# Reordering the two mixers of a hybrid decoder: earlier attention scores, convolution taps at the gate's input, later norm factors and V transposes

## The chip, the cores and the metric

One core of a Trainium2 chip runs the whole program. The metric is the device time of one execution in microseconds (us); lower is better. Times of the kernel before are the median of three runs; its profile is one execution taken by the hardware profiler.

## The reference

Sixteen learned meta tokens are put ahead of 512 tokens of width 1024 (528 positions), and two layers are computed, each a mixer and an MLP, both with a norm ahead of them and one behind them. The output leaves the meta tokens out.

```python
a = rmsnorm(h, mix_pre_g[l])
proj = a @ w_in[l]                  # q 512, k 128, v 128, b 512, c 512, h 512
q = partial_rope(q, cos, sin); k = partial_rope(k, cos, sin)
y_attn = sliding_window_gqa_sinks(q, k, v, sinks[l])   # 8 q heads, 2 kv heads, window 128
y_conv = b_gate * conv(c_gate * hc, conv_w[l])         # depthwise, causal, 3 taps
y = concat(rmsnorm(y_attn, attn_out_g), rmsnorm(y_conv, conv_out_g))
h = h + rmsnorm(y @ w_out[l], mix_post_g[l])
m = rmsnorm(h, mlp_pre_g[l])
h = h + rmsnorm(relu(m @ w_up[l])**2 @ w_down[l], mlp_post_g[l])
```

All of it is float32. A softmax row of `y_attn` holds a query's 128 keys and one sink, which only adds to its denominator.

## The kernel before, in words

Activations lie transposed: 128 features on the partitions, tokens on the free axis, split into RA (tokens 0 to 271) and RB (272 to 527). In layer 1 the outputs of the meta tokens are not wanted any more, so most of its products take 256 or 258 columns of RA.

A float32 product is made of three passes on TensorE (PE): every weight tile and activation is split into a high part (ScalarE copies it, L107 for weights) and a low remainder (VectorE subtracts, L108), and L192 to L194 multiply high by high, low by high and high by low. One product, 128 outputs of one range, has eight pieces of the contraction and so 24 matmuls. "Cast" below means the pair L107/L108 for half a weight tile (128x512); all weights are cast on the chip, each while earlier products run.

A mixer runs in these stages:

- `first_tiles` (L412): the products of K, V and three of the four Q tiles for RA, then for RB, while the end of the layer's previous stage still delivers activations piece by piece (`Post.step`, L309, writes `a_lo` at L334). V's product is transposed back to token order by `later()` in `v_evac` (L584) and split into `vv`; `v_later[0]` and `v_later[1]` are these for RA and RB.
- `mixer` (L630) walks a list `plan` of 26 products: the fourth Q tile for RA and RB, then for two pairs of channels four products each of the conv's c gate, its input h and its b gate. Between them, by the table `between` that `put` fills, go the pieces of attention. For each of eight pairs n of a block of 128 queries and a kv head: S[n] the scores (eight matmuls, four masks with a row maximum on VectorE, four exps on ScalarE, and, one product later, the scaling of the four score blocks by the reciprocal sum, L655), T[n] eight transposes on PE (L695) and a split, A[n] the product with V. `SCORES_AT` is the index of the product behind which S[0] goes, and `PERIODS` the distances from one T to the next.
- The conv: `c_evac` (L754) scales the c gate into `us[j]`, `h_evac` (L762) multiplies the h product into it, and `b_evac` takes the three taps (three scaled copies on ScalarE, L773 and L776, two additions on VectorE, L777), multiplies by the b product (L779) and adds the square to the norm's sum (`add_sq`, L266: a square on ScalarE, an addition on VectorE, L276).
- `group_norm` (L783): a factor from the sum of squares (two matmuls with a tile of ones, L231; three activations; L244, L245), then for each of four tiles a multiplication with gain and factor (L795), a high copy on ScalarE and a low remainder (L798).
- the out-projection (L883): products on all eight normed tiles, the four of attention first, then the four of the conv (`act_y`). The first four products on RA run together, piece by piece of the contraction, 12 matmuls for each piece, and the norms of RB are put between these pieces as hooks (`{1: ..., 3: ...}`: behind the piece of that number).

`pend` is a list of closing steps that wait until the next product has been issued. The program is written as such a sequence, and a scheduler then fixes the order of each engine's instructions; the order it came to is what the chip runs. Each engine works through its own list in order, so an instruction that waits holds up all behind it.

Of the kernel before, what the change touches and what calls it, by code (L numbers as in the profile page):

```python
# [10 lines left out]
AF = mybir.ActivationFunctionType  # L11
ALU = mybir.AluOpType
# [8 lines left out]
NCH = 4  # L21
CAP, PCAP = 7, 5
NA = 5
SCORES_AT = 7
PERIODS = (2, 3, 2, 3, 2, 2, 2, 2)
EPS = 1e-6
NEG = -1.0e30
RA = (0, 272)
# [3 lines left out]
G_PRE, G_ATT, G_CONV, G_POST, G_MPRE, G_MPOST, G_CW, G_N = 0, 8, 12, 16, 24, 32, 40, 52  # L32
# [3 lines left out]
def trunk_kernel(ctx, tc, xT, gains, sinkb, sinkm, rope, masks, maskm, ident_in, w_in, w_out, w_up, w_down, outT):  # L36
    nc = tc.nc
    ACT, DVE, POOL, PE = nc.scalar, nc.vector, nc.gpsimd, nc.tensor
# [11 lines left out]
    def tmp(w=272):  # L50
        return tp.tile([P, 272], F32, tag="t", name="t", bufs=8)[:, :w]

    h = cp.tile([P, KT, L], F32, name="h")
    z = cp.tile([P, KT, L], F32, name="z")
# [10 lines left out]
    gt = cp.tile([P, 2, G_N], F32, name="gt")  # L65
# [112 lines left out]
    def wtiles(n):  # L178
        return [wtile() for _ in range(n)]
# [6 lines left out]
    def tile_done(most=9):  # L186
        taken[0] -= size(done[0])
        done[0] += 1
        refill(most)
# [23 lines left out]
    def gemm(item, act):  # L213
        for ev in mms([item], act):
            ev()
# [31 lines left out]
    def utile():  # L247
        return tp.tile([P, L + 2], F32, tag="u", name="u", bufs=2)
# [4 lines left out]
    pend = []  # L253

    def flush():
        while pend:
            pend.pop(0)()
# [28 lines left out]
    def pre_rstd(r, name):  # L286

        t0, t1 = r  # L290
        w = meansq(accs["h"][:, t0:t1], 0)
        if name not in held:
            hold(name)
        acc = accs[name][:, t0:t1]
        if name == "c":
            chain(w, rt[:, t0:t1])
            ACT.activation(acc, w, AF.Identity, scale=-8 * EPS, bias=epst[:, 2:3])
        else:
            ACT.activation(acc, w, AF.Square, scale=-2 * (8 * EPS) ** 0.5, bias=epst[:, 1:2])
# [112 lines left out]
    def first_tiles(act, pB, rA, rB, nxt):  # L412


        items, tables, after, pcap, norm = nxt
        w = wtiles(NA)
        iA, iB = items(w, 0), items(w, 1)
        evs = []

        def rstd_a():  # L420
            pre_rstd(rA, norm)
            tables(0)

        initial = isinstance(pB, Start)
        at = (2, 4) if initial else (3, 5)
        groups = [(i,) for i in range(NA)] if initial else [(0, 1, 2), (3,), (4,)]
        steps = iter(range(4))
        for group in groups:
            i = group[0]
            hooks = {}  # L430
            if i == 0:
                hooks = {1 if initial else 4: pB.start}
            if i == at[0]:
                hooks = {at[1]: rstd_a}
            if not initial:
                evs += mms([iA[j] for j in group], act, hooks)
            elif i == 0:
                evs += mms(iA[:2], act)
            elif i >= 2:
                evs += mms([iA[i]], act, hooks)  # L440

            ready = [evs] if initial else [evs[:3]] if i == at[0] else [[ev] for ev in evs]
            if i >= at[0]:
                for run in ready:
                    waiting = pend[:]
                    pend.clear()
                    for ev in run:
                        ev()
                    for f in waiting:
                        f()  # L450
                evs = [] if initial else evs[3:] if i == at[0] else []
            for n in (0, 1)[:1 if len(group) == 1 else 2]:
                m = next(steps, None)
                if m is not None:
                    pB.steps(m)
            after(group[-1])
        cap[0] = pcap
        evs = mms(iB[:3], act)
        pre_rstd(rB, norm)
        tables(1)  # L460
        flush()
        for ev in evs:
            ev()
            tile_done()
        for i in range(3, NA):
            waiting = pend[:]
            pend.clear()
            gemm(iB[i], act)
            for f in waiting:
                f()  # L470
            tile_done()
# [23 lines left out]
    def xrange(l):  # L495
        return (RA if l == 0 else XA, RB)
# [27 lines left out]
    class Mixer:  # L524
# [8 lines left out]
        def tables(self, n):  # L533

            t0, t1 = (RA, RB)[n]
            nc.sync.dma_start(ct[:, t0:t1], rope[0][:, t0:t1])
            nc.sync.dma_start(st[:, t0:t1], rope[1][:, t0:t1])
            ACT.activation(r2[:, t0:t1], rt[:, t0:t1], AF.Square)
            DVE.tensor_tensor(ct[:, t0:t1], ct[:, t0:t1], rt[:, t0:t1], ALU.mult)
            DVE.tensor_tensor(st[:, t0:t1], st[:, t0:t1], rt[:, t0:t1], ALU.mult)  # L540
            for sw in sws:
                POOL.memset(sw[:, t0:t1], 0.0)
# [78 lines left out]
        def items(self, w, n):  # L621
            r = (RA, RB)[n]
            return [(w[0], r, self.k_evac(n)), (w[1], r, self.v_evac(n)),
                    ] + [(w[2 + j], self.xr[n], self.q_evac(j, n)) for j in range(NA - 2)]

        def after(self, i):
            if i == NA - 1:
                self.v_later[0]()

    def mixer(l, mx, mlp_first):  # L630

        xr = xrange(l)
# [112 lines left out]
        us = {}  # L745
# [11 lines left out]
        def h_evac(j, r):  # L757
            t0, t1 = r

            def ev(ps):  # L760
                u = us[j][:, 2 + t0:2 + t1]
                DVE.tensor_tensor(u, u, ps, ALU.mult)  # L762
            return ev

        def b_evac(j, r):
            t0, t1 = r

            def ev(ps):
                n = t1 - t0
                w = [gt[:, l, G_CW + 4 * x + j:G_CW + 4 * x + j + 1] for x in range(3)]  # L770
                u = us[j]
                t = tmp(n)
                ACT.activation(t, u[:, 2 + t0:2 + t1], AF.Copy, scale=w[2])  # L773
                for x in (1, 0):
                    t2 = tmp(n)
                    ACT.activation(t2, u[:, x + t0:x + t1], AF.Copy, scale=w[x])  # L776
                    DVE.tensor_tensor(t, t, t2, ALU.add)  # L777
                y = z[:, 4 + j, t0:t1]
                DVE.tensor_tensor(y, t, ps, ALU.mult)  # L779
                add_sq("c", j == 0, y, r)  # L780
            return ev

# [30 lines left out]
        def attn_norm(n):  # L813
            return group_norm(0, 4, "a", G_ATT, xr[n])

        def conv_norm(n):
            return group_norm(4, 0, "c", G_CONV, xr[n])

        def at_once(steps):
            return lambda: [f() for f in steps]  # L820

        plan = [("q", j, n) for j in range(NA - 2, 4) for n in range(2)]
        for jp in range(2):
            for kind in "chb":
                t = [(kind, 2 * jp + m, n) for m in range(2) for n in range(2)]
                if kind == "b" and jp == 1:
                    t = [t[0], t[2], t[1], t[3]]
# [3 lines left out]
        def put(i, *fs):  # L831
            between.setdefault(i, []).extend(fs)
# [2 lines left out]
        S = [lambda i=i, g=g: scores(i, g) for i, g in order]  # L835
        T = [lambda i=i, g=g: transp(i, g) for i, g in order]
        A = [lambda i=i, g=g: attend(i, g) for i, g in order]
        put(1, mx.v_later[1])
        at = SCORES_AT
        put(at, S[0])  # L840
        put(at + 1, S[1])
# [4 lines left out]
        pos = at + 3  # L846
        for n in range(8):
            put(pos, T[n])
            put(pos + 1, A[n])
            if n == 3:  # L850
                put(pos + 1, lambda: attn_sums(xr[0]))
                put(pos + 3, *attn_norm(0))
            if n == 7:
                put(pos + 1, lambda: attn_sums(RB))
            if n + 2 < 8:
                put(pos + 1, S[n + 2])
            pos += PERIODS[n]
        put(len(plan) - 2, *conv_norm(0))
        tiles = {}
        for i, (kind, j, n) in enumerate(plan):  # L860
            if (kind, j) not in tiles:
# [13 lines left out]
        for i in sorted(between):  # L875
            for f in between[i]:
# [8 lines left out]
        refill()  # L885
        w = wtiles(6)
        evs = mms([(w[m], xr[0], z_evac(m, xr[0], False, True, (l, G_POST))) for m in range(4)], act_y,
                  {1: at_once(attn_norm(1)), 3: at_once(conv_norm(1))})
        for ev in evs:
            ev()  # L890
        for m in range(4, 6):
# [9 lines left out]
    def f_evac(m, r):  # L901
        t0, t1 = r

        def ev(ps):
            f = tmp(t1 - t0) if t1 - t0 <= 272 else utile()[:, :t1 - t0]
            DVE.tensor_scalar(f, ps, 0.0, None, ALU.max)
            ACT.activation(f, f, AF.Square)
            split(f_hi[:, m, t0:t1], f_lo[:, m, t0:t1], f)
        return ev
# [73 lines left out]

    def mlp_items(l):
        xr = xrange(l)
        return (lambda w, n: [(w[m], xr[n], f_evac(m, xr[n])) for m in range(NA)]), (lambda n: None), (lambda i: None), CAP, "z"

    def mlp(l, nxt, first):

# [33 lines left out]
            POOL.memset(t[:, :, :PAD].bitcast(F32), 0.0)  # L1023

    m0, m1 = Mixer(0), Mixer(1)
    first = [(m.items, m.tables, m.after, PCAP, "c") for m in (m0, m1)]
    sA, sB = Start(0, 0, RA, (0, 0)), Start(0, 0, RB, (0, 0))
    prep((lambda: sA.load(0), lambda: sA.steps(0), lambda: sA.load(1), lambda: sA.steps(1)))
    prep((lambda: sA.load(2), lambda: sA.steps(2), lambda: sA.load(3), lambda: sA.steps(3)))
# [77 lines left out]
```

## Time and profile before

| | us |
|---|---|
| median of 3 runs | 1130.06 |
| lowest and highest | 1129.5, 1130.84 |
| the profiled execution | 1129.28 |
| its span (first to last instruction) | 1127.5 |
| PE busy | 1083.7 (96%), 8066 matmuls and transposes |
| VectorE (DVE) busy | 821.8 (73%) |
| ScalarE (ACT) busy | 640.3 (57%) |
| mean granted clock of PE | 0.983 |

Times in the rows are microseconds from the start of the span. A matmul is listed with its whole duration, though the next one starts long before it ends: what one costs in a row of many is the distance between starts. The clock is given as a share of the full 2.4 GHz; 0.5 is the lower level, 1.2 GHz. "Idle before" is the time for which the engine stood still ahead of the row's instruction, and behind the arrow is what ended it.

### The profile page before, as it was taken

Reading aid. Unit: us, or ns where it says so; the run is one execution under the profiler, and the core shown is the slowest. Engines: PE = TensorE matmul, PEld = TensorE weight load, DVE = VectorE, ACT = ScalarE, POOL = GpSimd, SP = SyncE. Lnnn points to the kernel's source line nnn. Section 1 sums busy time; section 2 is a strip of 40 time slices with the busy share of each in tenths; the row PEclk is TensorE's granted clock in tenths of the full one; section 3 lists DMA queues with packets and bytes.
Section 4 is the critical chain, followed back from the end, with each engine's and each line's share of the span. In section 5 each row is a group of like instructions: output and inputs, shape, how many; then the busy total and the mean of one; then the engine's idle time right before and its main releaser. Section 6 shows DMA issues by size and latency. Waiting matters only on the chain.

```text
span 1127.5 us, 21429 instructions
## 1 busy us (share of the span) xinstructions
PE 1083.7 (96%) x8066; PEld 1039.0 (92%) x8066; DVE 821.8 (73%) x1943; ACT 640.3 (57%) x1542; POOL 11.1 (1%) x46
## 2 busy tenths in 40 slices
PE   9999889999999999999979998899999999999996
PEld 8999889999999999999978998799888988988995
DVE  7987867978486586586588888779955856856835
ACT  8665766665473274275356556666834724724732
POOL 2000000000000000000000000000000000000000
PEclk9999989999999999999999999899999999999998
DMA  8342122342243243144132321222422522522502
GB/s 248 85 130 60 38 75 59 93 131 71 61 130 97 66 123 113 49 121 132 38 93 60 106 75 39 76 67 85 131 75 73 152 75 68 157 75 69 147 1 75
DMA packets 197608, 102.04 MB, mean 91 GB/s; under 512 B 7360, under 2 KB 197456, under 8 KB 197504
## 3 DMA queue, kind: packets, MB, share of 16 engines
q1 hardware_dynamic: 196640, 99.88, 30.5%
q8 instruction: 63, 1.03, 0.4%
q10 hardware_dynamic: 688, 0.58, 0.1%
q14 instruction: 41, 0.34, 0.1%
q0 software_dynamic: 176, 0.21, 0.1%
HBM read 97.88 MB, written 2.10 MB: 89 GB/s over the span
## 4 chain that ended last, share of the span: by engine, by line
PE 87%; DVE 8%; ACT 3%; issue 1%; DMA 1%; SPq 0%; DVEq 0%; ACTq 0%
PE ps L194 27%; PE ps L193 27%; PE ps L192 27%; PE ps L198 2%; DVE acc L276 1%; PE ps L231 1%; DVE a_lo L334 1%; PE ps L695 1%; DVE h L323 1%; DVE wlo L108 1%; ACT S L649 1%; DMA h<-in_xT 0%; DVE t L320 0%; DVE p L280 0%; DVE t L322 0%
## 5 line engine op out<-in xcount | busy, mean ns | idle before, releaser
L193 PE MATMUL ps<-f_lo,whi 128*128 128x256 f32 (+2 forms) x1072 | 325.9, 305 | 0.0
L194 PE MATMUL ps<-f_hi,wlo 128*128 128x256 f32 (+2 forms) x1072 | 325.0, 305 | 0.0
L192 PE MATMUL ps<-f_hi,whi 128*128 128x256 f32 (+2 forms) x1072 | 323.5, 306 | 0.0
L193 PE MATMUL ps<-a_lo,whi 128*128 128x256 f32 (+3 forms) x808 | 234.7, 293 | 2.3 <-DVE a_lo L334 2.1
L192 PE MATMUL ps<-a_hi,whi 128*128 128x256 f32 (+3 forms) x808 | 231.7, 298 | 4.5 <-ACT a_hi L329 3.4
L194 PE MATMUL ps<-a_hi,wlo 128*128 128x256 f32 (+3 forms) x808 | 233.1, 291 | 0.0
L193 PEld LDWEIGHTS ps<-f_lo,whi 128*128 128x128 f32 x1072 | 201.6, 188 | 9.6
L194 PEld LDWEIGHTS ps<-f_hi,wlo 128*128 128x128 f32 x1072 | 201.8, 189 | 9.2
L192 PEld LDWEIGHTS ps<-f_hi,whi 128*128 128x128 f32 x1072 | 200.0, 188 | 9.4
L108 DVE TENSOR_TENSOR wlo<-wraw,whi 128x512 fp32r<-128x512 f32 x264 | 173.7, 688 | 44.6 <-ACT whi L107 23.2
L107 ACT ACTIVATE whi<-wraw 128x512 fp32r<-128x512 f32 x264 | 153.4, 622 | 87.9 <-PE ps L193 59.6
L193 PEld LDWEIGHTS ps<-a_lo,whi 128*128 128x128 f32 x808 | 156.2, 193 | 6.6 <-DVE a_lo L334 3.6
L192 PEld LDWEIGHTS ps<-a_hi,whi 128*128 128x128 f32 x808 | 152.3, 193 | 8.7 <-ACT a_hi L329 4.9
L194 PEld LDWEIGHTS ps<-a_hi,wlo 128*128 128x128 f32 x808 | 156.5, 194 | 1.4 <-DVE wlo L108 0.2
L507 DVE TENSOR_TENSOR z<-z,ps 128x272 f32<-128x272 f32 (+2 forms) x78 | 38.0, 487 | 100.1 <-PE ps L194 99.9
L193 PE MATMUL ps<-a_lo,wf 128*128 128x264 f32 (+1 forms) x384 | 107.9, 282 | 0.0
L107 ACT ACTIVATE wf<-wraw 128x512 fp32r<-128x512 f32 x96 | 59.7, 626 | 84.8 <-PE ps L193 51.7
L192 PE MATMUL ps<-a_hi,wf 128*128 128x264 f32 (+1 forms) x384 | 107.7, 282 | 0.0
L194 PE MATMUL ps<-a_hi,wf 128*128 128x264 f32 (+1 forms) x384 | 107.1, 282 | 0.0
L107 ACT ACTIVATE wf<-u 128x512 fp32r<-128x512 f32 x72 | 45.2, 628 | 88.1 <-PE ps L193 73.6
L108 DVE TENSOR_TENSOR wf<-wraw,wf 128x512 fp32r<-128x512 f32 x96 | 65.8, 689 | 11.6 <-ACT wf L107 10.4
L193 PEld LDWEIGHTS ps<-a_lo,wf 128*128 128x128 f32 x384 | 72.2, 188 | 0.1
(176 smaller groups left out, 1826.1 us busy)
## 6 DMA issues: line engine op xcount, KB each, us to landing
wraw<-in_w_up SPq DMA_DIRECT2D x128, 256.0 KB
wraw<-in_w_down SPq DMA_DIRECT2D x128, 256.0 KB
wraw<-in_w_in SPq DMA_DIRECT2D x72, 256.0 KB
wraw<-in_w_out SPq DMA_DIRECT2D x32, 128.0 KB
wraw<-in_w_out SPq DMA_DIRECT2D x16, 256.0 KB
h<-in_xT SPq DMA_DIRECT2D x4, 272.0 KB
h<-in_xT SPq DMA_DIRECT2D x4, 256.0 KB
outT<-h SPq DMA_DIRECT2D x8, 128.0 KB
```

The costliest lines, as they stand in the source:

```text
L107: ACT.activation(hi, raw, AF.Copy)
L108: DVE.tensor_tensor(lo, raw, hi.bitcast(F32), ALU.subtract)
L192: PE.matmul(ps, whi, ahi, start=first, stop=False, skip_group_check=onto)
L193: PE.matmul(ps, whi, alo, start=False, stop=False, skip_group_check=onto)
L194: PE.matmul(ps, wlo, ahi, start=False, stop=last, skip_group_check=onto)
L198: PE.matmul(ps, a[n], b[n], start=first and n == 0, stop=last and n == 1)
L231: PE.matmul(ps, ones[:, which, :], acc, start=True, stop=more is None)
L276: return (eng or DVE).tensor_tensor(acc, acc, sq, ALU.add)
L323: DVE.tensor_tensor(hk, hk, t, ALU.add)
L334: DVE.scalar_tensor_tensor(a_lo[:, k, t0:t1], hk, g, a_hi[:, k, t0:t1].bitcast(F32), ALU.mult, ALU.subtract)
L507: DVE.tensor_tensor(zz, zz, ps, ALU.add)
L649: ACT.activation(S[:, i, keys], S[:, i, keys], AF.Exp, bias=ng[:, i:i + 1], accum_out=dn[:, i:i + 1])
```

## The change

The scores start behind the fifth product of the plan, where it was the eighth, with other distances between the transposes; all eight pairs are so done some products before the plan's end. The taps move from `b_evac` to a closing step of `h_evac`; two of the three scaled copies on ScalarE are dropped, since VectorE now multiplies and adds in one instruction. The hook `after` of `first_tiles`, which transposed V of RA at its end, is gone: both V transposes stand in the plan, behind its first and third product. The attention norm of RA comes one product later, the conv norm of RA moves from the plan's last products into the out-projection's first hook, and the two norms of RB move to later hooks.

```diff
-SCORES_AT = 7
-PERIODS = (2, 3, 2, 3, 2, 2, 2, 2)
+SCORES_AT = 4
+PERIODS = (2, 2, 3, 2, 2, 3, 2, 2)
...
-            after(group[-1])
...
-        def after(self, i):
-            if i == NA - 1:
-                self.v_later[0]()
...
-                u = us[j][:, 2 + t0:2 + t1]
-                DVE.tensor_tensor(u, u, ps, ALU.mult)
+                u = us[j]
+                DVE.tensor_tensor(u[:, 2 + t0:2 + t1], u[:, 2 + t0:2 + t1], ps, ALU.mult)
+
+                def taps():
+                    w = [gt[:, l, G_CW + 4 * x + j:G_CW + 4 * x + j + 1] for x in range(3)]
+                    first = max(t0, xr[0][0])
+                    y = z[:, 4 + j, first:t1]
+                    ACT.activation(y, u[:, 2 + first:2 + t1], AF.Copy, scale=w[2])
+                    for x in (1, 0):
+                        DVE.scalar_tensor_tensor(y, u[:, x + first:x + t1], w[x], y, ALU.mult, ALU.add)
+                pend.append(taps)
...
-                n = t1 - t0
-                w = [gt[:, l, G_CW + 4 * x + j:G_CW + 4 * x + j + 1] for x in range(3)]
-                u = us[j]
-                t = tmp(n)
-                ACT.activation(t, u[:, 2 + t0:2 + t1], AF.Copy, scale=w[2])
-                for x in (1, 0):
-                    t2 = tmp(n)
-                    ACT.activation(t2, u[:, x + t0:x + t1], AF.Copy, scale=w[x])
-                    DVE.tensor_tensor(t, t, t2, ALU.add)
                 y = z[:, 4 + j, t0:t1]
-                DVE.tensor_tensor(y, t, ps, ALU.mult)
+                DVE.tensor_tensor(y, y, ps, ALU.mult)
                 add_sq("c", j == 0, y, r)
...
-        put(1, mx.v_later[1])
+        put(0, mx.v_later[0])
+        put(2, mx.v_later[1])
...
-                put(pos + 3, *attn_norm(0))
+                put(pos + 4, *attn_norm(0))
...
-        put(len(plan) - 2, *conv_norm(0))
...
-                  {1: at_once(attn_norm(1)), 3: at_once(conv_norm(1))})
+                  {0: at_once(conv_norm(0)), 4: at_once(attn_norm(1)), 6: at_once(conv_norm(1))})
```

The rows below are the orders of the engines' instructions (line, operation, output<-inputs, shape, and a count where equal ones follow each other). Lines of the changed kernel are up to five lower than those of the kernel before.

VectorE in layer 0 around the first softmax (S and mx: scores and their row maximum; wlo: the low half of a weight cast; u: a tile of c gate by h; names carry the scheduler's tile numbers). Before:

```order
L108 TENSOR_TENSOR wlo_1139<-wraw_1142,whi_1138 128x512
L644 TENSOR_TENSOR mx_1019<-mx_1019,sb_78 128x4
L645 TENSOR_SCALAR ng_1035<-mx_1019 128x4
L646 TENSOR_TENSOR se_1037<-sb_78,mx_1019 128x4
L762 TENSOR_TENSOR u_917<-u_917,ps_1046 128x272
L660 ISA S_1078,mx_1079<-ps_1081,mk_82 128x144
```

With the change:

```order
L639 TENSOR_TENSOR mx_921<-mx_921,sb_78 128x4
L108 TENSOR_TENSOR wlo_1104<-wraw_1105,whi_1103 128x512
L757 TENSOR_TENSOR u_840<-u_840,ps_1018 128x272
L655 ISA s_1050,mx_1051<-ps_1053,mkm_83 64x16
L655 ISA mx_1051 64x1
L108 TENSOR_TENSOR wlo_1104<-wraw_1107,whi_1103 128x512
L655 ISA s_1050,mx_1051<-ps_1057,mkm_83 64x16
L655 ISA mx_1051 64x1
L639 TENSOR_TENSOR mx_991<-mx_991,sb_78 128x4
L640 TENSOR_SCALAR ng_937<-mx_921 128x4
L641 TENSOR_TENSOR se_939<-sb_78,mx_921 128x4
```

Before, the sink's maximum (L644) was followed at once by the negated maximum that the exps need (L645); now two casts, a multiplication of the conv, the two masks of the meta tokens and the maximum of the second pair stand between these two (L639, L640).

VectorE at the end of layer 0's mixer, up to the conv norm of RA (z: conv or attention outputs; acc: sum of squares; L244 and L245 before are the norm's factor, L795 its four multiplications). Before:

```order
L655 TENSOR_SCALAR S<-S,dn 128x256 x4
L276 TENSOR_TENSOR acc<-acc,t 128x272
L777 TENSOR_TENSOR t<-t 128x256 x2
L779 TENSOR_TENSOR z<-t,ps 128x256
L276 TENSOR_TENSOR acc<-acc,t 128x256
L244 SCALAR_TENSOR_TENSOR t<-ps,t 128x272
L245 SCALAR_TENSOR_TENSOR s<-t 128x272
L795 SCALAR_TENSOR_TENSOR t<-z,gt,s 128x272 x4
```

With the change:

```order
L703 TENSOR_TENSOR z<-ps,p 64x4x128
L774 TENSOR_TENSOR z<-z,ps 128x256
L108 TENSOR_TENSOR wlo<-wraw,whi 128x512 x4
L276 TENSOR_TENSOR acc<-acc,t 128x256 x3
L108 TENSOR_TENSOR wlo<-wraw,whi 128x512
L276 TENSOR_TENSOR acc<-acc,t 128x256
L108 TENSOR_TENSOR wlo<-wraw,whi 128x512
L244 SCALAR_TENSOR_TENSOR t<-ps,t 128x272
L245 SCALAR_TENSOR_TENSOR s<-t 128x272
L790 SCALAR_TENSOR_TENSOR t<-z,gt,s 128x272 x4
```

Before, the scaling of the last scores and tap additions stood right ahead of the norm's factor; now there are no taps and no scores left there, and six casts and four additions of squares stand ahead of it.

PE at the start of layer 1, where V of RA is transposed (u: V's product; ps: the accumulators). Before:

```order
L192 MATMUL ps_7771<-a_hi_70,whi_7475 128x256
L193 MATMUL ps_7771<-a_lo_71,whi_7475 128x256
L194 MATMUL ps_7771<-a_hi_70,wlo_7476 128x256
L584 MATMUL ps_7853<-ident_85,u_7746 128x128 x3
L192 MATMUL ps_7859<-a_hi_70,whi_7087 128x256
```

With the change:

```order
L192 MATMUL ps_8050<-a_hi_70,whi_7491 128x256
L193 MATMUL ps_8050<-a_lo_71,whi_7491 128x256
L194 MATMUL ps_8050<-a_hi_70,wlo_7492 128x256
L583 MATMUL ps_8089<-ident_85,u_7706 128x128 x3
L192 MATMUL ps_8095<-a_hi_70,whi_7491 128x256
```

The transposes (L584, now L583) stood ahead of the five products of RB; now they stand in the plan, 139 rows of PE's order later.

## Rows read from the trace of the kernel before

**Rows 1.** Windows: stretch, its us, busy us of PE, PEld, DVE, ACT, POOL, clock, DMA.

```profile
24.00:64.00 40.00, 39.56 (x328) 39.33 (x327) 37.69 (x94) 26.52 (x67) 1.08 (x4) 1.00 0.35 96
60.00:110.00 50.00, 50.00 (x405) 49.19 (x405) 42.66 (x154) 32.07 (x94) 0.20 (x2) 1.00 0.35 101
110.00:125.00 15.00, 12.72 (x89) 12.06 (x88) 11.35 (x38) 10.87 (x32) 0.00 (x0) 0.89 0.16 48
125.00:150.00 25.00, 20.07 (x138) 18.95 (x137) 21.05 (x68) 17.88 (x50) 0.00 (x0) 0.86 0.15 43
690.00:720.00 30.00, 23.56 (x172) 22.13 (x171) 26.71 (x82) 21.09 (x57) 0.00 (x0) 0.89 0.18 51
683.00:686.00 3.00, 1.27 (x9) 1.09 (x9) 1.59 (x7) 2.17 (x10) 0.00 (x0) 1.00 0.60 175
```

**Rows 2.** Timeline of PE, tails of both mixers: start, us, instruction, idle before.

```profile
119.26 1.25 PE L231 MATMUL ps<-acc,ones 128*128 128x272 f32 x2 [2.28 <-DVE acc L276]
...
144.79 1.27 PE L231 MATMUL ps<-acc,ones 128*128 128x272 f32 x2 [4.13 <-DVE acc L276]
...
684.84 0.67 PE L231 MATMUL ps<-acc,ones 128*128 128x256 f32 x2 [1.73 <-DVE acc L276]
...
704.24 1.14 PE L695 MATMUL ps<-ident,S 128*128 128x128 f32 x8 [1.89 <-DVE S L655]
...
709.49 1.22 PE L231 MATMUL ps<-acc,ones 128*128 128x256 f32 x2 [4.11 <-DVE acc L276]
```

**Rows 3.** Timeline of PE at the first score matmul of layers 0 and 1.

```profile
64.68 0.28 PE L198 MATMUL ps<-k_hi,f_hi 128*128 128x256 f32 x1
...
632.98 0.28 PE L198 MATMUL ps<-k_hi,f_hi 128*128 128x256 f32 x1
```

**Rows 4.** Timeline of VectorE around the first softmax of layers 0 and 1.

```profile
64.68 0.44 DVE L762 TENSOR_TENSOR u<-u,ps 128x272 f32<-128x272 f32 x1
65.04 1.89 DVE L108 TENSOR_TENSOR wlo<-wraw,whi 128x512 fp32r<-128x512 f32 x3
...
67.06 0.44 DVE L777 TENSOR_TENSOR t<-t 128x272 f32<-128x272 f32 x1
67.42 0.41 DVE L762 TENSOR_TENSOR u<-u,ps 128x256 f32<-128x256 f32 x1
...
68.10 0.30 DVE L660 CUSTOM_DVE_ANT_0 S<-ps,mk 128x144 f32<-128x144 f32 x1
...
68.33 0.30 DVE L660 CUSTOM_DVE_ANT_0 S<-ps,mk 128x144 f32<-128x144 f32 x1
...
70.41 0.17 DVE L645 TENSOR_SCALAR ng<-mx 128x4 f32<-128x4 f32 x1
...
72.45 0.17 DVE L652 TENSOR_TENSOR dn<-dn,se 128x4 f32<-128x4 f32 x1 [0.35 <-ACT S L649]
...
632.59 0.42 DVE L762 TENSOR_TENSOR u<-u,ps 128x258 f32<-128x258 f32 x1
```

**Rows 5.** Groups of VectorE, 20 to 160 us: count, busy us, mean ns, idle before.

```profile
L660 DVE CUSTOM_DVE_ANT_0 S<-ps,mk 128x256 f32<-128x256 f32 x24 | 8.9, 422 | 2.6 <-PE ps L198 2.6
L655 DVE TENSOR_SCALAR S<-S,dn 128x256 f32<-128x256 f32 x24 | 6.8, 349 | 0.1
L795 DVE SCALAR_TENSOR_TENSOR t<-z,gt,s 128x272 f32<-128x272 f32 x8 | 3.5, 498 | 0.1
```

**Rows 6.** Timelines of PE and VectorE at the start of layer 1.

```profile
587.73 0.88 PE L584 MATMUL ps<-ident,u 128*128 128x128 f32 x3 [5.99 <-DVE u L578]
...
599.80 0.48 DVE L334 SCALAR_TENSOR_TENSOR a_lo<-h,gt,a_hi 128x256 fp32r<-128x256 f32 x1
...
600.34 0.58 PE L193 MATMUL ps<-a_lo,whi 128*128 128x256 f32 x1 [0.45 <-DVE a_lo L334]
```

**Rows 7.** Timeline of VectorE, conv norm of RA in layer 0.

```profile
147.84 0.44 DVE L244 SCALAR_TENSOR_TENSOR t<-ps,t 128x272 f32<-128x272 f32 x1 [0.87 <-ACT t L243]
...
152.00 0.43 DVE L798 TENSOR_TENSOR f_lo<-t,f_hi 128x272 fp32r<-128x272 f32 x1
```

## What the change was forecast to do

> **What bounds the kernel now.** The table of busy times comes first: PE is at work nearly all the time and VectorE three quarters of it, so time is to be had only where PE waits or runs at the lower clock. The view of windows finds these places. From 60 to 110 us, the middle of layer 0's mixer, PE has no gap: 50.00 us, 405 instructions, 0.123 us each, clock 1.00 [rows 1]. Behind it, from 110 to 150, it is busy for 32.79 of 40 us, at 0.89 and 0.86 of the clock; layer 1 shows the same at 690 to 720 (23.56 of 30, at 0.89). PE's timeline says what it waits for there [rows 2]: the sums of squares (L276) of the attention norm of RA (2.28 us at 119.26, 1.73 at 684.84) and of the conv norm of RA (4.13 at 144.79, 4.11 at 709.49), and in layer 1 the last scores (1.89 at 704.24). These are tails: the plan runs out of products while VectorE still works on softmax, taps and norms.
>
> What the two tails cost: in layer 0 the idle time is 2.28 + 4.93 = 7.2 us, and the clock costs 12.72 x 0.11 + 20.07 x 0.14 = 1.4 + 2.8 us, together **11.4**. In layer 1 the idle time is 1.73 + 6.44 = 8.2, the clock 23.56 x 0.11 = 2.6, together **10.8** [rows 1].
>
> VectorE decides elsewhere too. From 24 to 64 us it is busy for 37.69 of 40 [rows 1], so there is no room in it where layer 0's scores are now to be moved.
>
> **The change part by part.** *PE's work* is not changed: the same products, scores, transposes and norm sums. *Taps:* per product ScalarE loses two copies and VectorE has two scale-and-add instructions in place of two additions. A three-operand form takes 0.498 us [rows 5], an addition 0.44 (the one at 67.06 [rows 4]): 16 instructions a mixer, 0.06 each, 1 us of VectorE spread over 70 us, taken as nothing on PE. What counts is that the taps no longer stand ahead of the conv norm.
>
> *The tails.* Scores, transposes and attention end three products earlier (the periods' sum is the same 18), so the last transposes are covered by products; between the sums and the factor of RA's attention norm lies one product more (24 x 0.123 = 3.0 us), which covers 2.28 and 1.73; the waits for conv sums lose the taps ahead of them. I count both tails as gone, **22.2 us**, and count the new waits below against them.
>
> *The first softmax of layer 0.* PE has eight products of the plan ahead of S[0] now, and with the change eight ahead of the first transposes, T[0]. So it reaches T[0] where it now starts S[0], plus S[0] and S[1] and the meta tokens' scores: 64.68 [rows 3] + 16 matmuls x 0.115 + 0.2 = 66.7. VectorE comes later. At 64.68 it starts the first conv multiplication (L762) [rows 4]; of what it did before, only a c multiplication (0.34, from the distance of 67.06 to 67.42) and two casts (0.63 each, from 1.89 for three) now stand behind the first mask. So the first mask starts at 64.68 - 1.6 = 63.1, though PE could deliver the scores long before. To the negated maximum come eight masks at 0.225 (the distance of 68.10 to 68.33), 1.8; five casts, 3.1; a c and an h multiplication, 0.7; meta masks and small operations 0.5: 69.2. From the negated maximum to the sum behind the four exps took 2.04 us (70.41 to 72.45 [rows 4]), reciprocal and two scalings add 0.7: S[0] is ready at 72.0. **A wait of 5.3 us**, where there was none. Its bounds: 0, if the scheduler's order is not what holds the masks back, and 7, if a cast also waits for a weight buffer that PE frees at 66.9.
>
> What a wait does to the clock: after the 2.28 us at 119.26 the clock of the stretch is 0.89, after the 1.73 us at 684.84 it is 1.00 [rows 1, 2]. I charge waits above 2 us with 1.4, as in 110 to 125: **1.4** here. The Trainium skill, page "TensorE: Matmul & The Clock Gate", section "HAM oscillation — how this bites in real kernels", lets only idle gaps longer than the 2.28 us seen here throttle PE. By that rule the wait for T[6] below would cost no clock and the sum would be 1.4 less; the trace differs, for a shorter wait was followed by a lower clock.
>
> *T[6] of layer 0.* In the new order S[6] is followed closely by T[6]. Between the splits of T[5] and T[6] PE has 58 product matmuls, 8 scores and 4 of A, the latter twice as wide: 74 x 0.123 = 9.1 us, say 8.9 with the narrower ones. VectorE has in that piece four masks (0.42 each by their mean, 0.35 back to back), eight scalings (0.35, 0.27 back to back), ten three-operand instructions of taps and norm (0.498, 0.41 back to back) [rows 5], four casts (2.5), eight plain operations of 0.34 (2.7) and small ones (0.5): 1.4 + 2.1 + 4.1 + 5.7 - 2.0 (what lies behind the first two scalings and ahead of the splits) = 11.3, and ScalarE's copy 0.7 ahead of it. 12.0 - 8.9 = **3.0 us**, and **1.4** of clock. By the means instead of the back-to-back times the wait is 4.5, and 0 if VectorE stands ahead when the piece begins.
>
> *Conv norm of RA.* It is now a hook behind the first piece of the out-projection, used from the fifth on: 36 matmuls, 4.5 us of cover. The chain from the norm's sum to the first low remainder took 7.2 us (144.79 to 152.00 [rows 2, 7]), with taps and casts between; unhidden that leaves 2.7, with its queue of 2 us gone 0.7; six casts now stand ahead of it. I take **1.0** in each layer (0 to 2.7), nearer the lower end, since PE's 1.27 us for the sum was at the lower clock.
>
> *Layer 1's first softmax.* PE is at T[0] at 632.98 [rows 3] + 1.8 = 634.8. VectorE has slack there. Its h multiplication, at 632.59 [rows 4], is pushed by the eight masks (1.8) and small ones (0.3) to 634.7; multiplication, reciprocal and two scalings behind it make 636.0: **1.2 us**. T[6] there has fewer operations ahead (no meta tokens, the norm of a narrower RA): 0.3, and 0.3 to 0.4 for split waits in each layer.
>
> *V transposes.* The 5.99 us wait of L584 at 587.73 [rows 6] looks like a gain. But the products of RB behind it need `a_lo`, which VectorE delivers piece by piece up to 599.80, and PE waits again at 600.34 for just that. VectorE's chain is not shortened by PE being early, so a wait saved at 587.73 comes back at the next pieces: **0**, bounds +1 (a late RA) and -8 (the wait and its lower clock truly gone).
>
> *Sum:* -22.2; layer 0 +5.3 +1.4 +3.0 +1.4 +1.0 +0.3 = 12.4; layer 1 +1.2 +0.3 +1.0 +0.4 = 2.9; net **-6.9 us**. The profiled execution, 1129.28 (span 1127.5), becomes 1122.4; the median of the runs is 0.78 above it, so I predict **1123.2**.
>
> **The rivals.** *Both tails go and nothing takes their place.* The order is taken up by buffers in flight and T[0] and T[6] of layer 0 find their scores ready. For: 60 to 110 us is without a gap. Against: VectorE's 37.69 of 40 just ahead. About 2 us of waits are left in each layer: -18.2, 1111.9.
>
> *The V wait truly goes.* If VectorE's work on `a_lo` is held up by the V split itself, freeing PE frees it as well. Against: the chain up to 599.80 has no split in it. Up to 8 us more than the forecast, 1115.
>
> *Gains and new waits cancel.* The wait at T[0] and T[6] is at its upper bound with the clock (7 + 4.5 + 2.8) and layer 1's conv norm at 2.7, or the change moves the tails without removing them: -6.9 + 1.7 + 1.5 + 2 x 1.7 = -0.3, no change.
>
> *VectorE becomes the bound in both layers (slower).* Place: T[0] of layer 1. If S[0] there is ready more than 3 us after 634.8, layer 1 repeats layer 0: 5.3 + 1.4 + 3.0 + 1.4 + 2.7 = 13.8 in place of 10.8, and layer 0 with the longer waits (7 + 1.4 + 4.5 + 1.4 + 2.7 = 17.0) stands against 11.4: +8.6, 1138.7. For: the scores move to where casts and rope are done. Against: layer 1 has no meta tokens and VectorE waits for PE at that place now.
>
> **How the numbers follow.** Forecast 0.57, its own range 1118 to 1128; nothing in the tails' place 0.13; V wait gone 0.08; cancel 0.13; VectorE the bound 0.09. A measurement of this kernel can tell 0.2%, 2.3 us, from no change: faster is below 1127.8. The first three cases are faster, 0.78; cancel is the same, 0.13; the last slower, 0.09. The range leaves out half of the second case at its lower end and the last case, with part of the fourth, at the upper: 1112 to 1129.5.
>
> **What would show it.** Right: no wait above 1 us at L231 in the mixers; a wait of PE at the first L690 of layer 0 of about 5 us and at a later one of about 3, ended by VectorE's L650; layer 1's first L690 about 1 us; the waits for `a_lo` at 588 to 600 as long in sum as before, under other lines. Wrong: no wait at the first L690 of layer 0, waits of L690 in layer 1 above 3 us, or a start of layer 1 that is shorter by more than 1 us.

## The result and the profile after

The changed kernel takes 1121.16 us (median of four runs, 1120.94 to 1121.7) against 1129.78 for the kernel before in the same comparison: a ratio of 0.9923, 95% interval 0.9909 to 0.9938, or 8.6 us less. Forecast were 6.9 us less, 1123.2, in a range of 1112.0 to 1129.5. The span of the profiled executions fell from 1127.5 to 1119.2 us, by 8.3.

The windows of the changed kernel, with the columns of [rows 1], show where the tails went (64 to 110 is there for a sum below):

```profile
24.00:64.00 40.00, 40.00 (x334) 39.95 (x333) 38.29 (x104) 26.79 (x68) 1.08 (x4) 1.00 0.34 93
60.00:110.00 50.00, 45.67 (x352) 44.47 (x351) 41.89 (x152) 29.27 (x87) 0.20 (x2) 0.97 0.29 83
64.00:110.00 46.00, 41.67 (x319) 40.47 (x317) 37.98 (x139) 27.11 (x83) 0.20 (x2) 0.96 0.26 76
110.00:125.00 15.00, 15.00 (x121) 14.65 (x120) 13.36 (x46) 10.13 (x27) 0.00 (x0) 1.00 0.18 50
125.00:150.00 25.00, 21.66 (x160) 21.11 (x159) 20.59 (x58) 13.49 (x39) 0.00 (x0) 0.93 0.15 43
690.00:720.00 30.00, 28.97 (x225) 27.55 (x224) 25.31 (x68) 17.58 (x45) 0.00 (x0) 1.00 0.36 104
```

From 110 to 125 and from 690 to 720, where PE lost 2.28 and 6.44 us and a tenth of the clock [rows 1], it now works almost without a gap at the full clock. In exchange the stretch from 60 to 110, once without a gap, loses 4.33 us and some of the clock. None of the five waits of [rows 2] is left. In their place PE's timeline has these waits of 0.9 us or more in the two mixers:

```profile
71.41 0.41 PE L690 MATMUL ps<-ident,S 128*128 128x128 f32 x2 [4.33 <-DVE S L650]
...
135.45 0.41 PE L690 MATMUL ps<-ident,S 128*128 128x128 f32 x2 [3.34 <-DVE S L650]
...
651.53 0.44 PE L690 MATMUL ps<-ident,S 128*128 128x128 f32 x2 [1.28 <-DVE S L650]
...
656.83 0.50 PE L198 MATMUL ps<-p,vv 128*128 128x512 f32 x1 [1.35 <-ACT p L279]
...
694.31 0.41 PE L690 MATMUL ps<-ident,S 128*128 128x128 f32 x2 [0.95 <-DVE S L650]
```

The first two are T[0] and T[6] of layer 0. Each of the four that stand at a transpose (L690) ends with VectorE's scaling of scores (L650, which was L655 before).

VectorE's timeline around the first softmax of layer 0 answers to [rows 4]: the last mask of S[0] (63.38), the maximum with the sink, the negated maximum, the sum behind the exps, the scaling:

```profile
63.38 0.30 DVE L655 CUSTOM_DVE_ANT_0 S<-ps,mk 128x144 f32<-128x144 f32 x1
...
66.66 0.15 DVE L639 TENSOR_TENSOR mx<-mx,sb 128x4 f32<-128x4 f32 x1
...
68.54 0.15 DVE L640 TENSOR_SCALAR ng<-mx 128x4 f32<-128x4 f32 x1
...
70.56 0.16 DVE L647 TENSOR_TENSOR dn<-dn,se 128x4 f32<-128x4 f32 x1 [0.29 <-ACT S L644]
...
70.97 0.90 DVE L650 TENSOR_SCALAR S<-S,dn 128x144 f32<-128x144 f32 x4
```

Five us pass between the last mask and the negated maximum, though nothing but the order holds it back: the queue has five casts, the masks of S[1] and of the meta tokens and two multiplications of the conv there.

Around T[6] the same queue shows it more plainly. The sum for S[6] (L647) is there at 128.43, but its reciprocal (L648) comes at 132.03 and the scaling at 134.96, behind the masks of S[7], taps, remainders and casts:

```profile
128.43 0.15 DVE L647 TENSOR_TENSOR dn<-dn,se 128x4 f32<-128x4 f32 x1
...
129.96 0.41 DVE L655 CUSTOM_DVE_ANT_0 S<-ps,mk 128x256 f32<-128x256 f32 x1
...
132.03 0.17 DVE L648 RECIPROCAL dn<-dn 128x4 f32<-128x4 f32 x1
...
133.35 1.28 DVE L108 TENSOR_TENSOR wlo<-wraw,whi 128x512 fp32r<-128x512 f32 x2
...
134.96 1.14 DVE L650 TENSOR_SCALAR S<-S,dn 128x256 f32<-128x256 f32 x4
```

At the start of layer 1, PE's timeline answers to [rows 6]. The wait of 5.99 us for V is gone, and others stand in its place:

```profile
583.29 0.39 PE L192 MATMUL ps<-a_hi,whi 128*128 128x256 f32 x1 [0.63 <-ACT t L549]
...
586.01 0.39 PE L193 MATMUL ps<-a_lo,whi 128*128 128x256 f32 x1 [0.69 <-DVE a_lo L334]
...
588.73 0.38 PE L193 MATMUL ps<-a_lo,whi 128*128 128x256 f32 x1 [1.22 <-DVE a_lo L334]
...
597.25 1.01 PE L192 MATMUL ps<-a_hi,whi 128*128 128x256 f32 x3 [7.54 <-ACT a_hi L329]
```

### The profile page after: what moved, and what is told of

Its sections match the earlier page's. It is cut to its first block, busy times and chain, and to the rows that moved or that the text cites. A ratio compares the mean times of both kernels' runs of the same rounds, so it can differ in the third digit from the quotient of the medians.

```text
span 1119.2 us, 21378 instructions
## 1 busy us (share of the span) xinstructions
PE 1079.4 (96%) x8066; PEld 1035.5 (93%) x8066; DVE 821.4 (73%) x1943; ACT 627.7 (56%) x1510; POOL 11.2 (1%) x46
## 4 chain that ended last, share of the span: by engine, by line
PE 83%; DVE 10%; ACT 2%; DMA 2%; issue 1%; SPq 1%; DVEq 0%; ACTq 0%
PE ps L192 26%; PE ps L194 26%; PE ps L193 26%; PE ps L198 2%; DVE wlo L108 2%; PE ps L690 1%; DMA wraw<-in_w_in 1%; DVE a_lo L334 1%; DVE h L323 1%; DVE acc L276 1%; PE ps L231 1%; DMA h<-in_xT 1%; SPq L554 1%; DMA z<-t 0%; DVE S L655 0%
## 5 line engine op out<-in xcount | busy, mean ns | idle before, releaser
L108 DVE TENSOR_TENSOR wlo<-wraw,whi 128x512 fp32r<-128x512 f32 x264 | 173.3, 687 | 49.9 <-ACT whi L107 27.5
L108 DVE TENSOR_TENSOR wf<-wraw,wf 128x512 fp32r<-128x512 f32 x96 | 65.8, 688 | 11.1 <-ACT wf L107 10.1
```

Source lines behind the costliest of these rows:

```text
L108: DVE.tensor_tensor(lo, raw, hi.bitcast(F32), ALU.subtract)
```

## The experiments

Each was timed beside the kernel before on the same chip (its medians: 1130.03, 1129.91 and 1129.92 in the three groups of four), and every ratio is to that. Waits, windows and starts are from one profiled execution of each. Each edit lets the scheduler lay out VectorE's list anew, so a run compares whole orders and not only the part that was edited.

**First group: one part of the change undone.**

*V transposes back.* `put(0, mx.v_later[0])` and `put(2, mx.v_later[1])` give way to the old hook:

```diff
+            after(group[-1])
...
-        put(0, mx.v_later[0])
-        put(2, mx.v_later[1])
+        put(1, mx.v_later[1])
```

> The changed kernel with the V transposes alone put back: RA's behind the products of first_tiles, RB's behind the plan's second product. Theory (VectorE's delivery of a_lo sets the start of layer 1): the wait of L584 for V of about 6 us comes back, the waits for a_hi and a_lo behind it shrink by as much, their sum at the start of layer 1 stays at 8.5 to 10 us, and the time is that of the change, 1121.2, within 1.0. Rival (the V transposes carry part of the gain): 1124 or more.

1120.84 us, ratio 0.9919 (0.9906 to 0.9931): the same as the change. The wait for V is back, and the one behind it is smaller by 4.6 us:

```profile
586.37 0.87 PE L584 MATMUL ps<-ident,u 128*128 128x128 f32 x3 [5.99 <-DVE u L578]
...
597.92 1.01 PE L192 MATMUL ps<-a_hi,whi 128*128 128x256 f32 x3 [2.92 <-ACT a_hi L329]
```

Together 8.9 us against 10.1 with the change. The V transposes are worth nothing in the total, as the first theory had it. But layer 0 is not left as it was, which neither theory had:

```profile
70.23 0.41 PE L695 MATMUL ps<-ident,S 128*128 128x128 f32 x2 [1.57 <-DVE S L655]
...
142.55 0.44 PE L695 MATMUL ps<-ident,S 128*128 128x128 f32 x2 [2.02 <-DVE S L655]
```

T[0] waits 1.57 us in place of 4.33 and T[6] not at all; T[3] waits 1.70, T[7] 2.02, and four shorter waits make the sum from 20 to 165 us 7.8, against 7.7 with the change.

*Conv norm back.*

```diff
+        put(len(plan) - 2, *conv_norm(0))
...
-                  {0: at_once(conv_norm(0)), 4: at_once(attn_norm(1)), 6: at_once(conv_norm(1))})
+                  {1: at_once(attn_norm(1)), 3: at_once(conv_norm(1))})
```

> The changed kernel with the norms of the conv and of RB alone put back: conv norm of RA behind the plan's last product but one, norms of RB at hooks 1 and 3. Theory (the waits of 4.1 us for the conv's sums went because the taps no longer stand behind the last b products, not because the norm is used later): no wait above 1 us at the conv norm's sums, 1121 to 1123.5. Rival (the later place of the norm removed these waits): waits of 3 to 4 us come back in both layers, with clock 1128 to 1131.

1127.75 us, ratio 0.9982 (0.9973 to 0.9991). Theory and rival both missed the time. The wait for the conv's sums did not come back, so the norm's later place is not needed to remove it; but 6.6 us of the gain are lost. Most of it is in layer 1's out-projection, where PE now waits for ScalarE's copy of normed tiles:

```profile
720.72 0.74 PE L192 MATMUL ps<-f_hi,whi 128*128 128x256 f32 x4 [2.33 <-ACT f_hi L792]
...
721.79 0.70 PE L231 MATMUL ps<-acc,ones 128*128 128x256 f32 x2 [0.33 <-DVE acc L276]
```

and loses 0.06 of the clock from 715 to 745 us (27.34 us busy, so 1.6 us; 1.00 with the change). The hooks of RB's norms, which were put back with it, are part of this; the two were not tried apart.

*Taps back.* The taps stand in `b_evac` again, as in the removed lines of the change's diff.

> The changed kernel with the taps alone put back into the b gate's evacuation. Theory (the waits at the first transposes and at T[6] come from VectorE's order, in which taps are a small part, and the conv norm has 7 us of cover in the out-projection): T[0] still waits 4 to 5 us, T[6] 2.5 to 4, the conv norm's wait in layer 0 is below 2 us; 1121 to 1125. Rival (the taps at the b gate are what made the tails wait): conv norm waits of 3 us or more in both layers, 1127 to 1131.

1126.54 us, ratio 0.9966 (0.9954 to 0.9978), between the two ranges. T[0] waits 5.32 us, T[6] not at all (T[7] waits 1.56), RB's sums wait 1.79 in layer 0. So T[6]'s wait, which the theory had expected to stay, went here as it went with the V transposes back: it belongs to the whole order and not to one part. The b gate's taps alone do not bring the 4.1 us waits back, which the rival wanted. The loss lies in layer 1, with 1.95 and 2.32 us at transposes and 1.10 at the sums.

*Scores back.*

```diff
-SCORES_AT = 4
-PERIODS = (2, 2, 3, 2, 2, 3, 2, 2)
+SCORES_AT = 7
+PERIODS = (2, 3, 2, 3, 2, 2, 2, 2)
```

> The changed kernel with SCORES_AT 7 and the old PERIODS. Theory (early scores cost 4.3 and 3.3 us of waits and 3 of clock in layer 0, while the taps and the later norms alone remove most of the tails' waits): no wait at T[0] nor T[6] of layer 0, a wait of 2 to 4 us for the last scores' transposes in each layer; faster than the change, 1113 to 1119. Rival (the early scores are what empties the tails): the tails' waits for the last scores grow to 5 us or more in both layers, 1124 to 1130.

1133.44 us, ratio 1.0036 (1.0023 to 1.005): slower than the kernel before. The theory fell. The rival's direction held, but not its range (1124 to 1130) nor its place: T[7], the last scores' transposes, waits 2.56 us in layer 0 and not at all in layer 1. T[0] and T[6] are rid of their waits (0.94 at T[0]), but PE waits at the sums of the attention norm and of RB, in layer 1 for

```profile
689.50 0.70 PE L231 MATMUL ps<-acc,ones 128*128 128x256 f32 x2 [4.32 <-DVE acc L276]
...
724.89 2.07 PE L231 MATMUL ps<-acc,ones 128*128 128x256 f32 x4 [2.84 <-DVE acc L276]
```

Nearly all of the loss is in layer 1: its first sums come at 573.07, against 572.87 with the change.

**Second group: VectorE's order, and parts alone.**

*Both behind.* On the changed kernel, the scheduler is told to issue VectorE's part of a cast behind the first softmax's negated maximum, and masks behind the last scaling (`first_ng` holds the one, `scaled` the other; the first line stands ahead of L108's subtraction in `cast`, the second ahead of the reduction in `masked`):

```diff
+        with tc.issue_after(first_ng[0].ins) if first_ng else nullcontext():
...
+            with tc.issue_after(scaled[0].ins) if scaled else nullcontext():
...
```

> The changed kernel; VectorE's order alone is altered: the casts are queued behind the first softmax's negated maximum, and every mask behind the last scaling issued in the program before it. Theory (the waits at T[0] and T[6] of layer 0 come from what the order puts ahead of the negated maximum and of the scaling, not from the work itself): the wait at T[0] falls from 4.3 to below 1.5 us, that at T[6] from 3.3 to below 1, and with the clock's 1.7 and 1.5 the time falls to 1111 to 1115. Rival (VectorE has no room there, so the work set back makes the next transposes or products wait as long): 1119 to 1123, with new waits at T[1] or at casts.

1122.88 us, ratio 0.9937 (0.9923 to 0.9951): the rival, at another place than it named. T[0] waits 1.97 in place of 4.33, T[6] 1.70 in place of 3.34, but the transposes of the meta tokens, whose masks were set back as well, wait 1.89:

```profile
69.05 0.60 PE L695 MATMUL ps<-ident,S 128*128 128x128 f32 x2 [1.97 <-DVE S L655]
...
81.28 0.27 PE L727 MATMUL ps<-ident,s 64*128 64x64 f32 x1 [1.89 <-DVE s L655]
...
134.98 0.44 PE L695 MATMUL ps<-ident,S 128*128 128x128 f32 x2 [1.70 <-DVE S L655]
```

and in layer 1 another 1.45 and 1.44 us appear.

*Masks behind.* The second of these two edits alone.

> The changed kernel; on VectorE every mask is queued behind the last scaling issued in the program before it, and nothing else is altered. Theory: the wait at T[6] of layer 0 falls from 3.3 to below 1.5 us with its 1.5 us of clock, T[0] still waits 3 to 5 us; 1116 to 1119. Rival (no room on VectorE): waits at other transposes take its place, 1120 to 1123.

1125.06 us, ratio 0.9961 (0.9949 to 0.9974), above both ranges. In layer 0 T[6]'s wait fell to 0.87 us with the clock at 1.00 from 125 to 150, and the first sums of layer 1 come 2.3 us earlier (570.61 for 572.87). Layer 1 takes 6.4 us more, the largest part of it at one wait:

```profile
658.47 0.79 PE L198 MATMUL ps<-p,vv 128*128 128x512 f32 x1 [3.29 <-ACT p L279]
```

Later masks gave later exps there, and these stand ahead of ScalarE's copy of `p`.

*Scores alone*, on the kernel before: the two lines of numbers of the change.

> The kernel before with SCORES_AT 4 and the new PERIODS alone; taps at the b gate, norms and V transposes as they were. Theory (the parts depend on each other: early scores bring the waits at T[0] and T[6], and without the later norms and the earlier taps the waits for the conv's sums stay): 1128 to 1134, with a wait above 2 us for the conv's or RB's sums in both layers. Rival (the early scores carry the gain by themselves): 1120 to 1125.

1127.42 us, ratio 0.9976 (0.9967 to 0.9984), a little below the theory's range. T[0] waits only 1.39, about as little as in the run with the V transposes back; here too they stand at their old place. The other wait the theory named is there in another form, at the conv's normed tiles instead of their sums:

```profile
159.28 0.77 PE L192 MATMUL ps<-f_hi,whi 128*128 128x272 f32 x4 [3.59 <-ACT f_hi L797]
...
721.03 0.74 PE L192 MATMUL ps<-f_hi,whi 128*128 128x256 f32 x4 [2.42 <-ACT f_hi L797]
```

*Transposes later* (layer 0):

```diff
-        pos = at + 3
+        pos = at + (4 if l == 0 else 3)
```

> The changed kernel with the transposes and the later scores of layer 0 one product (3 us) later, S[0] and S[1] where they are. Theory (S[0] is ready at 71.0 whatever PE does): the wait at T[0] falls from 4.3 to 1.3 to 1.8 us and its clock cost goes; T[6] keeps 2 to 3.5 us; 1116 to 1119. Rival (the tail of layer 0 needs that product): waits of 2 us or more come back at the last transposes or at the norms' sums of layer 0, 1120 to 1124.

1115.93 us, ratio 0.988 (0.9867 to 0.9894): better than both kernels, and at the lower edge of the theory's range. The parts were off: T[0] waits 2.13 (forecast 1.3 to 1.8), T[6] 1.43 (2 to 3.5). RB's sums now wait 2.18 us, the rival's wait, at less than it gains. PE's timeline, and windows of layer 0 with the full clock:

```profile
71.53 0.41 PE L690 MATMUL ps<-ident,S 128*128 128x128 f32 x2 [2.13 <-DVE S L650]
...
131.90 0.41 PE L690 MATMUL ps<-ident,S 128*128 128x128 f32 x2 [1.43 <-DVE S L650]
...
153.59 1.10 PE L231 MATMUL ps<-acc,ones 128*128 128x256 f32 x4 [2.18 <-DVE acc L276]
```

```profile
64.00:110.00 46.00, 43.87 (x351) 42.79 (x350) 40.72 (x150) 28.47 (x89) 0.20 (x2) 1.00 0.28 81
...
125.00:150.00 25.00, 23.30 (x181) 22.43 (x180) 19.42 (x55) 13.29 (x32) 0.00 (x0) 1.00 0.22 65
150.00:160.00 10.00, 7.82 (x60) 7.53 (x59) 9.55 (x24) 7.51 (x21) 0.00 (x0) 1.00 0.36 106
```

**Third group.**

*Masks behind in layer 0 alone*: `if scaled and l == 0` in the edit above.

> The changed kernel with the masks queued behind the last scaling in layer 0 alone. Theory (this order saved 2.3 us in layer 0 and lost its gain in layer 1 only): T[6] of layer 0 waits below 1.5 us, layer 1 as in the change; 1118 to 1120. Rival (the loss came from anywhere else): 1121 to 1126.

1119.78 us, ratio 0.9907 (0.9893 to 0.9922), 1.4 below the change and inside the theory's range, though the two intervals overlap. The wait at T[6] is what tells:

```profile
70.44 0.66 PE L690 MATMUL ps<-ident,S 128*128 128x128 f32 x2 [3.12 <-DVE S L650]
...
133.17 0.41 PE L690 MATMUL ps<-ident,S 128*128 128x128 f32 x2 [0.87 <-DVE S L650]
...
142.43 0.44 PE L690 MATMUL ps<-ident,S 128*128 128x128 f32 x2 [1.04 <-DVE S L650]
```

T[6] lost 2.5 us of its wait with VectorE's work unchanged; T[7], which did not wait with the change, now waits 1.0.

*Both of these.* Transposes later and masks behind, in layer 0.

> The kernel with layer 0's transposes one product later, and masks queued behind the last scaling in layer 0 besides. Theory (the two waits have causes of their own, so the two gains add up where a wait is left): T[6]'s 1.4 us goes, T[0] keeps about 2 us; 1113 to 1116. Rival (one product more of cover is what both take): no gain over 1115.9, or a loss of 1 to 4 us with waits at T[1] or the meta tokens' transposes.

1123.6 us, ratio 0.9942 (0.9929 to 0.9956): the rival, and more. T[0]'s wait falls to 0.77, and T[6] waits for nothing, but the meta tokens' masks are caught by the same rule:

```profile
80.98 0.34 PE L722 MATMUL ps<-ident,s 64*128 64x64 f32 x1 [6.67 <-DVE s L650]
```

Whether the two add up with the meta tokens left out of the rule was not tried.

*Transposes later in both layers*: `pos = at + 4`.

> The changed kernel with the transposes one product later in both layers. Theory (layer 1's waits before its transposes were 1.3, 1.35 and 1.0 us at full clock): 1 to 2 us less in layer 1 than with layer 0's alone; 1114 to 1116. Rival (layer 1's tail, with fewer columns to hide it, needs the product): waits of 2 us or more at the last transposes or norm sums of layer 1; 1117 to 1121.

1115.62 us, ratio 0.987 (0.9856 to 0.9884), the same as with layer 0's alone: the time is in the theory's range, but the 1 to 2 us that it had for layer 1 are not there. The waits of layer 1's transposes went, and RB's sums wait in their stead:

```profile
710.47 1.13 PE L231 MATMUL ps<-acc,ones 128*128 128x256 f32 x4 [2.85 <-DVE acc L276]
```

*Taps alone*, on the kernel before.

> The kernel before with the taps alone moved to the gate's input. Theory (without early scores the tail still ends with the last scores and their sums, and the taps come to stand where VectorE works on softmax): the waits for the attention norm's sums stay at 2 us or more, those for the conv's sums fall from 4.1; 1127 to 1134. Rival (the taps at the b gate made the tails): both waits of 4.1 us gone, 1120 to 1124.

1132.01 us, ratio 1.0021 (1.0012 to 1.003): in the theory's range, and slower than the kernel before. The 4.1 us waits for the conv's sums [rows 2] are gone in both layers. The taps at the b gate are thus a condition of these waits, but not the whole cause, for with the scores alone they are gone at the sums too. The waits for the attention norm's sums, 2.28 and 1.73 before, grow:

```profile
121.29 0.70 PE L231 MATMUL ps<-acc,ones 128*128 128x272 f32 x2 [4.06 <-DVE acc L276]
...
687.04 1.19 PE L231 MATMUL ps<-acc,ones 128*128 128x256 f32 x2 [4.86 <-DVE acc L276]
```

and T[7], which did not wait before, waits 1.76 us in layer 0 and 3.08 in layer 1.

## Why the prediction was right, point by point

- **The tails, 22.2 us.** All five waits went, with their clock, and two beside them that I had not counted, of 0.64 and 0.95 us at the sums of the norm behind the mixer. (The 1.89 us at 704.24, which the prediction put down to the last scores, stood at T[6] of layer 1; T[7] did not wait.) The reason was given as if each part removed its own waits. The runs show that the parts need each other: taps alone 1132.0, scores alone 1127.4 (the later norms alone were not run), all but the scores 1133.4, all but the taps 1126.5, all but the later conv and RB norms 1127.8. Where one is left out, waits appear at other places. Nearly all of this is in layer 1. There, leaving out the scores, the taps or the norms costs 10.1, 5.0 and 4.9 us from the layer's first sums on; up to these sums it costs 0.2, 0.7 and 1.4, for in layer 0 the new waits at T[0] and T[6] take up most of what the tails gave.
- **T[0] of layer 0, 5.3 us and 1.4 of clock.** Measured 4.33 and 41.67 x 0.04 = 1.7 us (64 to 110). The steps were right in detail: first mask 62.70 for 63.1, negated maximum 68.54 for 69.2, first scaling 70.97, which I had done by 72.0. PE reached it at 67.1 for 66.7. What the forecast did not see is that the early scores alone do not make this wait: with the V transposes at their old place T[0] waits 1.57 us, and with the scores alone 1.39.
- **T[6], 3.0 us and 1.4.** Measured 3.34 and 21.66 x 0.07 = 1.5 us. The size was right and the reason half so. I put it down to the amount of VectorE's work, where the order decides: with S[7]'s masks behind S[6]'s scaling, the same work leaves 0.87, and 1.04 at T[7].
- **Conv norm of RA, 1.0 us in each layer: wrong, it is 0.** PE sums the squares at 153.86, the first low remainder starts at 160.95, and PE waits for neither:

```profile
153.86 0.62 PE L231 MATMUL ps<-acc,ones 128*128 128x272 f32 x2
...
160.95 0.79 DVE L793 TENSOR_TENSOR f_lo<-t,f_hi 128x272 fp32r<-128x272 f32 x2
```

I counted 36 matmuls of cover. PE's order has 24 more ahead of the conv's pieces, the attention pieces of two further products, so the cover is 60 matmuls, 7.5 us by the price I used.
- **Layer 1, +2.9 us.** The waits in its mixer sum to 1.28 + 1.35 + 0.95 = 3.6, but not where I had them: T[0] waits for nothing. Its h multiplication came at 632.13, which with the 2.03 us by which the layer starts earlier (572.87 for 574.90) is 634.2 for my 634.7, and the scalings followed at once.
- **V transposes, 0.** Right in the total, and at the start of layer 1 for the reason given, by a margin that [rows 6] alone didn't give: the wait at 597.25 ends 2.02 us earlier than its counterpart at 599.27 before, and the layer's first sums came 2.03 us earlier. Putting them back changes nothing in the total. In layer 0 the nearly equal sums of waits (7.8 and 7.7 us, at other transposes) are luck: the forecast had no term for what their place does there.
- **The sum.** Forecast were +1.0 in layer 0 and -7.9 in layer 1. In the profiled executions the change is 2.0 us ahead at the first sums of layer 1 and 8.3 at the end: -2.0 and -6.3. So two errors of 3.0 and 1.6 us partly cancel, and the closeness of the total is in part luck. In layer 0 the conv norm's 1.0, T[0]'s 0.7 net, 0.3 for a split and the uncounted 0.64 us make 2.6, of which T[6] takes back 0.4. Two more waits of the kernel before, 0.44 us at 26.07 and 0.43 at 152.86, went uncounted, and one at the start of layer 0 grew by 0.4; the 0.3 us that are left were not followed up. In layer 1 the waits at the start are longer by 1.6 us with the change (10.1 against 8.5), where 0 was forecast; they are about the size of the error there.

Of the rivals, that nothing takes the tails' place is excluded by the waits at T[0] and T[6], that the V wait truly goes by its run, and that gains and new waits cancel by the time, 1121.16, which lies below the 1127.8 that was set as faster. VectorE did not become the bound in layer 1: S[0] there made PE wait for nothing.

## What to carry to other kernels

When one engine's queue is nearly full, an edit that takes work off one wait can put it ahead of another. A part moved alone can then read as worse (the taps) while the set is better, so combinations have to be timed. Where a wait ends with a short operation, look how long its inputs had been ready: a gap there points to the order rather than the load, and a run with another order can test it. The cheapest cure here was not to reorder the full engine but to have the waiting one come a product later, which gave 5 us more.

## What the runs showed of the hardware

The lower clock does not follow from a wait's length alone. After waits of 2.28 us [rows 2], of 2.02 in the run with the V transposes back (142.55, 125 to 150 at 0.93) and of 2.19 with the scores alone (110 to 125 at 0.89) the clock was lower:

```profile
110.97 0.44 PE L695 MATMUL ps<-ident,S 128*128 128x128 f32 x2 [2.19 <-DVE S L655]
...
110.00:125.00 15.00, 14.03 (x99) 13.78 (x100) 12.92 (x43) 10.06 (x29) 0.00 (x0) 0.89 0.13 36
```

After 2.13 and 2.18 with the transposes later the windows show 1.00, and after 2.85 at 710.47 with the transposes later in both layers the window from 705 to 715 shows 1.00 too. So the charge of 1.4 us for every wait above 2 us was about right for T[0] and T[6] (1.7 and 1.5), and would have been wrong for those.

The Trainium skill, page "TensorE: Matmul & The Clock Gate", section "HAM oscillation — how this bites in real kernels", has only idle gaps longer than any of these throttle PE. The trace agrees for the 4.33 us (0.97 from 60 to 110) and speaks against it for the three waits of 2.02 to 2.28 us.
